# Segment mean on one core: boundaries of the rows from 66 on computed on ScalarE, two check parts moved to ScalarE, own columns placed in two parts

## The chip, the cores and the metric

The kernel runs on one core of a Trainium2 chip. The metric is the time on the device for one execution in microseconds; lower is better. The kernel before takes 188.7 us, the median of four runs (188.03 to 189.13).

## The reference

The input is ten million float32 values and ten million segment numbers (int64), sorted in ascending order, between 0 and 9999. The output is the mean of the values of each of the 10,000 segments:

```
sums = zeros(num_segments); counts = zeros(num_segments)
np.add.at(sums, segment_ids, data)
np.add.at(counts, segment_ids, 1)
return sums / np.maximum(counts, 1)
```

Since the numbers are sorted, a segment is one contiguous piece of the data. With about 1000 values in each, what has to be found is where one segment ends and the next begins, and the sum of the values between two such places.

## The kernel before

Each of the 128 partitions takes 78,125 consecutive values, cut into 90 rows of L = 875 (the last has 250). A row is shorter than a segment usually is, so it holds at most one boundary, and four things are done for it:

- **Probes.** SyncE loads every 175th segment number (`pr`, 8-byte elements, L163), two rows in one transfer. From the sum SG of a row's five probes VectorE finds in which piece of 175 the boundary lies (ST) and the address of that piece (IDX): `first_look`, six instructions for a group of six rows, L284 to L303. The last of them makes YY, the number of probes and their sum in one value.
- **Gather.** GpSimd fetches for each row the 175 numbers of that piece (`GT`, L317), one indirect transfer per row, into a ring of 18 rows. The six gathers of a group are issued as soon as `first_look` has their addresses.
- **Boundary.** ScalarE adds up the gathered numbers (`add_ids`, L327) into G in PSUM. VectorE then makes the boundary's place KK from YY and G (`second_look`, L334). It does this for six rows at once, and from row HALVES = 66 on for three. At the last row it also adds `tl`, which corrects for the shorter last row (L339).
- **Total and split.** ScalarE sums the row's values (`total`, L347), and VectorE sums the values ahead of KK (`split`, L352). Both read the data tile, which holds two rows (875 KB). SyncE loads the tiles, 26 rows ahead, in one queue with the probes (L171). The last tile comes in two transfers (L171, L173).

The order of the work is written out by hand. A loop at the kernel's end (L865 to L897) goes through the rows r. In row r it issues loads that are due; then the boundary sums of the rows up to r + x_sum (6 rows ahead, and 5 from row 66 on) on ScalarE; then `total(r)`, `split(r)`, and whatever the list `after[r]` holds. `put(r, steps, every)` writes steps into this list, `every` of them to a row. All engines run their own instructions in this order, and each waits only for what it needs.

The list holds the rest of the computation in pieces. `counts` turns boundaries into reciprocals of counts (L573 to L591). `sums` makes running sums (L598 to L610). `select` and `table` put the means of a partition's first rows into a table (L662, L671, L676). `place` moves the table's columns to the 79 segments that the partition owns (L686, L693). The columns that later rows reach are found by `pick` (masks, on GpSimd for the later rows: L703 to L718) and `spread` (L748, L751), whose product for rows 62 to 77 runs on GpSimd at L751 and is summed by VectorE at L759, behind row 83. `inject` adds the last two rows.

A check runs along: `check_frame`, `check_windows` (L528 to L532) and `check_columns` fill an array `bad`, `verdict` sums it (L557), adds it over the partitions on TensorE (L558) and makes a flag (L561). All engines load this flag into a register at L850, which stands in the list behind row 80. If it is set, a slow general path runs at the end; with this input it doesn't.

Of the kernel before, what the change touches and what calls it, by code (L numbers as in the profile page):

```python
# [17 lines left out]
P = 128  # L18
# [7 lines left out]
W = S  # L26
# [92 lines left out]
def kernel(  # L119
# [24 lines left out]
    def x_sum(r):  # L144
        return 6 if r < HALVES else 5

# [100 lines left out]
    def g_of(a, b):  # L247
        i = [(r // GROUPS[0] if r < HALVES else 1 + (r - HALVES) // 3) % 2 for r in range(a, b)]
        assert min(i) == max(i)
        return G[i[0]][:, a:b]  # L250
# [18 lines left out]
    def first_look(g):  # L269
# [28 lines left out]
        def s5():  # L298
            for c, d, w in [(a, b - 1, S), (b - 1, b, TAIL)] if last else [(a, b, S)]:
                v.scalar_tensor_tensor(  # L300
                    out=IDX[:, c:d], in0=ST[:, c:d], scalar=float(w), in1=wb[:, c:d], op0=ALU.mult, op1=ALU.add
                )
            v.scalar_tensor_tensor(  # L303
                out=YY[:, a:b], in0=ST[:, a:b], scalar=float(K + 1), in1=SG[:, a:b], op0=ALU.mult, op1=ALU.add
            )
            if last:
                v.tensor_scalar(
                    out=tl, in0=ST[:, NR - 1 : NR], scalar1=-1.0, scalar2=float(TAIL - S),
                    op0=ALU.add, op1=ALU.mult,
                )  # L310
            gather(g)
# [13 lines left out]

    def add_ids(r):
        nc.scalar.activation(  # L327
            out=junk_a, in_=gt32[:, r % RING, 0 : 2 * W : 2], func=ACT.Copy,
            accum_out=g_of(r, r + 1),
        )  # L330

    def second_look(a, b):
        def s1():
            nc.vector.scalar_tensor_tensor(  # L334
                out=KK[:, a:b], in0=YY[:, a:b], scalar=float(S // K), in1=g_of(a, b),
                op0=ALU.mult, op1=ALU.subtract,
            )
            if b == NR:
                nc.vector.tensor_add(out=KK[:, NR - 1 : NR], in0=KK[:, NR - 1 : NR], in1=tl)  # L339

        return [s1]
# [60 lines left out]
    bads = cpool.tile([P, 1], FP32, name="bads")  # L402
    badi = cpool.tile([P, 1], I32, name="badi")
    misc = ppool.tile([P, 512], FP32, name="misc")
    ext = misc[:, 0 : 5 * E + 1]
# [119 lines left out]
    def check_windows():  # L525
# [4 lines left out]
            ),  # L530
            lambda: v.tensor_mul(out=j2, in0=j1, in1=j1),
            lambda: v.scalar_tensor_tensor(  # L532
# [22 lines left out]
    def verdict():  # L555
        def s1():
            nc.vector.tensor_reduce(out=bads, in_=bad, axis=AX.X, op=ALU.add)  # L557
            nc.tensor.matmul(out=badp, lhsT=ones, rhs=bads, start=True, stop=True)  # L558
# [239 lines left out]
    for a, b in zip(bounds[1:], bounds[2:]):  # L798
        if a < HALVES:
            put(a - 1, second_look(a, b))  # L800
        else:
            put(a - 1, second_look(a, a + 3))
            put(a + 2, second_look(a + 3, b))
    for g in range(HEAD, NG):
# [3 lines left out]
    def mixed(p, q):  # L808
# [23 lines left out]
    put(59, counts(Q1, R1), 2)  # L832
    put(R1 - 1, mixed(sums(Q1, R1), select(H1, M1)) + table(H1, M1, tab), 2)
    put(64, place(0, T1, tab, [(0, C1, ND + 1, OUT[:, 0:C1]), (C1, T1, ND + 1, xa[:, 0 : T1 - C1, RM - R1])]))
    look = bounds[NG - 1] - X_LOOK - 2
# [9 lines left out]
    put(look + 1, edges_of(RE, NR))  # L845
    put(look + 4, single(0, NX, bad[:, NX:NC]) + verdict())
    put(look + 4, [
# [6 lines left out]
        + total_of(xa[:, C2 - C1 :, :], add[:, 0 : CA - C2, nb]))  # L854
    w = weights()
    put(RS - 2, counts(RM, R2) + w[:3], 99)
    block = sums(RM, R2, False, RS) + spread(RM, R2, pb, add[:, :, 0:nb], NO - C2) + total_of(add, most)
# [71 lines left out]
```

## Time and profile before

| | us |
|---|---|
| median of four runs | 188.7 |
| the profiled execution's own time | 187.97 |
| its span in the profile | 186.2 |
| VectorE (DVE) busy | 141.2 (76%) |
| ScalarE (ACT) busy | 116.9 (63%) |
| GpSimd (POOL) busy | 99.9 (54%) |
| splits, L352, 90 of them, mean 1118 ns | 100.6 |
| totals, L347, 90 of them, mean 931 ns | 83.8 |
| boundary sums, L327, 90 of them, mean 333 ns | 29.9 |
| gathers, L317, 90 of them, mean 1010 ns | 90.9 |

DMA moved 54.63 MB, a mean of 293 GB/s. The span is what the profile shows between the first and the last instruction; the execution's own time also has what lies around it. The profile cuts the span into 40 slices of equal length and gives for each the busy share of each engine in tenths. A line of the timeline gives start, length, engine, line, operation, tiles with their shapes, and in brackets how long the engine had been idle and what seems to have ended that. The reading out of a sum (READ_ACCUMULATOR) is an instruction of its own behind the one that sums. A busy share is a mean over stages, so the prediction takes the stages one by one.

### The profile page before, as it was taken

The numbers are of one execution on the slowest core, as the hardware profiler recorded it, in microseconds if no ns is written. First come the engines' busy times: TensorE is split into PE (matmuls) and PEld (weight loads), VectorE is DVE, ScalarE is ACT, GpSimd is POOL, SyncE is SP. The second block draws the span as 40 slices with busy tenths as digits, with TensorE's granted clock in tenths as the row PEclk, the third lists the DMA queues.
The fourth block names the chain that finished last, engine by engine and source line by source line (L and its number), as shares of the span: only waits on it lengthen the run. The fifth ranks groups of instructions, "written<-read, shape, count | busy, mean of one in ns | idle before, by whom it ended". The sixth has DMA issues, their size and how long they took to land.

```text
span 186.2 us, 1477 instructions
## 1 busy us (share of the span) xinstructions
PE 1.6 (1%) x6; PEld 1.4 (1%) x6; DVE 141.2 (76%) x438; ACT 116.9 (63%) x362; POOL 99.9 (54%) x119
## 2 busy tenths in 40 slices
PE   0000000000002000000000000000000000010000
PEld 0000000000001000000000000000000000010000
DVE  6522397989297697757799997567699989999991
ACT  8010488935988293873928748397585485959920
POOL 5578776086725728275282664707527478784000
DMA  6899999999999999999999999999998999999100
GB/s 31 175 154 351 336 330 329 316 330 328 330 327 301 340 341 308 322 321 322 330 306 333 328 330 314 298 344 305 325 279 232 330 403 403 410 405 399 60 0 12
DMA packets 70613, 54.63 MB, mean 293 GB/s; under 512 B 60464, under 2 KB 61032, under 8 KB 70599
## 3 DMA queue, kind: packets, MB, share of 16 engines
q1 hardware_dynamic: 64667, 40.50, 74.4%
q0 software_dynamic: 5760, 14.01, 23.0%
q14 instruction: 14, 0.11, 0.2%
q10 hardware_dynamic: 172, 0.00, 0.1%
HBM read 56.59 MB, written 0.04 MB: 304 GB/s over the span
## 4 chain that ended last, share of the span: by engine, by line
SPq 34%; DMA 23%; DVE 16%; issue 13%; POOL 7%; ACT 3%; POOLq 0%; ACTq 0%; DVEq 0%
SPq L171 26%; DMA GT<-in_segment_ids_dram,IDX 14%; DMA data_t<-in_data_dram 10%; DVE junk_v L352 8%; SPq L163 8%; POOL GT L317 6%; ACT junk_t L347 2%; ACT junk_a L327 1%; POOL xa L751 1%; DVE sel L671 1%; DVE shf L686 1%; POOL pb L717 0%; DVE ct L585 0%; DVE most L759 0%; DVE sel L662 0%
## 5 line engine op out<-in xcount | busy, mean ns | idle before, releaser
L317 POOL DMA_INDIRECT GT<-in_segment_ids_dram,IDX x90 | 90.9, 1010 | 67.4 <-ACT junk_a L327 33.8
L352 DVE SCALAR_TENSOR_TENSOR junk_v<-iota,q,data_t 128x875 bf16<-128x875 f32 x90 | 100.6, 1118 | 15.9 <-DMA data_t<-in_data_dram 14.5
L347 ACT ACTIVATE junk_t<-data_t 128x875 bf16<-128x875 f32 x90 | 83.8, 931 | 3.2 <-DMA data_t<-in_data_dram 2.8
L327 ACT ACTIVATE junk_a<-GT 128x175 f32<-128x175 int32 x90 | 29.9, 333 | 57.3 <-DMA GT<-in_segment_ids_dram,IDX 51.9
L347 ACT ACTIVATION_READ_ACCUMULATOR junk_t<-data_t 128x1 f32 x90 | 15.6, 174 | 0.0
L327 ACT ACTIVATION_READ_ACCUMULATOR junk_a<-GT 128x1 f32 x90 | 12.5, 139 | 0.0
L334 DVE SCALAR_TENSOR_TENSOR q<-YY,G 128x6 f32<-128x6 f32 (+1 forms) x19 | 2.9, 155 | 12.4 <-ACT junk_a L327 12.4
L352 DVE DVE_READ_ACCUMULATOR junk_v<-iota,q,data_t 128x1 f32 x90 | 7.4, 82 | 0.0
L284 DVE TENSOR_REDUCE SG<-pr 128x6 f32<-128x30 int32 x15 | 2.7, 180 | 5.3 <-DMA pr<-in_segment_ids_dram 5.2
L293 DVE TENSOR_SCALAR far<-ST 128x6 f32<-128x6 f32 x15 | 2.9, 195 | 0.5
L187 ACT ACTIVATE GT<-q 128x3150 int32<-128x3150 f32 x1 | 3.0, 2994 | 0.0
L300 DVE SCALAR_TENSOR_TENSOR IDX<-ST,wb 128x6 int32<-128x6 f32 (+2 forms) x16 | 2.6, 165 | 0.5
L296 DVE TENSOR_TENSOR ST<-ST,far 128x6 f32<-128x6 f32 x15 | 2.6, 170 | 0.5
L287 DVE SCALAR_TENSOR_TENSOR ST<-pr,SG 128x6 f32<-128x6 int32 x15 | 2.5, 166 | 0.5
L303 DVE SCALAR_TENSOR_TENSOR YY<-ST,SG 128x6 f32<-128x6 f32 x15 | 2.5, 168 | 0.0
L236 DVE CAST jj<-jj_i 128x128 f32<-128x128 int32 x1 | 1.5, 1483 | 0.7 <-POOL jj_i L235 0.7
L598 DVE TENSOR_TENSOR q<-T,q 128x44 f32<-128x44 f32 (+3 forms) x4 | 0.7, 174 | 1.7 <-ACT junk_t L347 1.6
L187 ACT ACT_TABLE_LOAD x1 | 1.3, 1283 | 0.7 <-PEq L913 0.7
L718 POOL TENSOR_SCALAR pb<-pb 128x168 f32<-128x168 f32 (+1 forms) x2 | 1.6, 784 | 0.2
L558 PE MATMUL misc<-bads,ones 128*128 128x1 f32 x2 | 0.6, 363 | 104.7 <-DVE bads L557 104.7
L558 PEld LDWEIGHTS misc<-bads,ones 128*128 128x128 f32 x2 | 0.5, 312 | 104.7 <-DVE bads L557 104.7
L585 DVE RECIPROCAL ct<-ct 128x16 f32<-128x16 f32 (+2 forms) x4 | 1.2, 300 | 0.1
(129 smaller groups left out, 44.9 us busy)
## 6 DMA issues: line engine op xcount, KB each, us to landing
data_t<-in_data_dram SPq DMA_DIRECT2D x44, 875.0 KB, 10.4
GT<-in_segment_ids_dram,IDX POOLq DMA_INDIRECT x90, 6.4
pr<-in_segment_ids_dram SPq DMA_DIRECT2D x41, 10.0 KB, 8.0
data_t<-in_data_dram SPq DMA_DIRECT2D x1, 437.5 KB, 18.6
data_t<-in_data_dram SPq DMA_DIRECT2D x1, 125.0 KB, 15.9
out_dram<-OUT SPq DMA_DIRECT2D x1, 36.6 KB
pr<-in_segment_ids_dram SPq DMA_DIRECT2D x1, 31.0 KB, 4.0
snt<-in_segment_ids_dram ACTq DMA_DIRECT2D x1, 1.0 KB
```

The lines of the kernel that those rows point to most:

```text
L163: nc.sync.dma_start(out=pr_flat[:, a:b], in_=ids_p[:, a * S : (b - 1) * S + 1 : S])
L171: nc.sync.dma_start(out=d[:, 0 : c - a], in_=data_p[:, a:c])
L187: nc.scalar.activation(out=gt32[:, :, 0 : 2 * W : 2], in_=view(q5[:, 0, 0:1], [[0, RING], [0, W]]), func=ACT.Copy)
L284: v.tensor_reduce(out=SG[:, a:b], in_=pr32[:, a:b, 0 : 2 * K : 2], axis=AX.X, op=ALU.add)
L293: v.tensor_scalar(out=far, in0=ST[:, a:b], scalar1=0.0, scalar2=FAR, op0=ALU.is_equal, op1=ALU.mult)
L296: v.tensor_add(out=ST[:, a:b], in0=ST[:, a:b], in1=far)
L300: v.scalar_tensor_tensor(out=IDX[:, c:d], in0=ST[:, c:d], scalar=float(w), in1=wb[:, c:d], op0=ALU.mult, op1=ALU.add)
L317: nc.gpsimd.indirect_dma_start(out=GT[:, r % RING, :], out_offset=None, in_=ids2d[:], in_offset=bass.IndirectOffsetOnAxis(ap=IDX[:, r : r ...
L327: nc.scalar.activation(out=junk_a, in_=gt32[:, r % RING, 0 : 2 * W : 2], func=ACT.Copy, accum_out=g_of(r, r + 1),)
L334: nc.vector.scalar_tensor_tensor(out=KK[:, a:b], in0=YY[:, a:b], scalar=float(S // K), in1=g_of(a, b), op0=ALU.mult, op1=ALU.subtract,)
L347: nc.scalar.activation(out=junk_t[:, 0:n], in_=d, func=ACT.Copy, accum_out=t)
L352: nc.vector.scalar_tensor_tensor(out=junk_v[:, 0:n], in0=iota[:, 0:n], scalar=KK[:, r : r + 1], in1=d, op0=ALU.is_lt, op1=ALU.mult, accum_ ...
```

## The change

- From row 66 on, ScalarE computes KK by itself: an activation with factor -1 and the bias YY of that row, whose sum over the 175 elements is written to KK. YY is made to fit in `first_look` by another operation of the same size. The second looks of these rows are gone, and the sums stand 4 rows ahead instead of 5. The addition of `tl` becomes a step of its own, ahead of the last `counts`.
- The square in `check_windows` and the sum of `bad` in `verdict` go from VectorE to ScalarE. The last step of the verdict (the flag) moves from behind row 79 to behind row 80, directly ahead of the register load.
- The columns of the first table are placed in two parts: 23 of them behind rows 50 and 51, the other 33 behind rows 65 and 66. Before, all 56 were placed behind rows 64 and 65.
- `select` of windows 5 to 7 goes from behind row 61 to behind row 60, and the sums and table of rows 44 to 61 begin behind row 62 instead of row 61.

```diff
--- before.py
+++ after.py
@@ -142,7 +142,7 @@
     ctx.enter_context(tc.manual_schedule())
 
     def x_sum(r):
-        return 6 if r < HALVES else 5
+        return 6 if r < HALVES else 4
 
 
     pr = cpool.tile([P, NR + 1, K], I64, name="pr")
@@ -245,7 +245,7 @@
     T = [ppool.tile([P, 512], FP32, name=f"T{i}") for i in range(2)]
 
     def g_of(a, b):
-        i = [(r // GROUPS[0] if r < HALVES else 1 + (r - HALVES) // 3) % 2 for r in range(a, b)]
+        i = [r // GROUPS[0] % 2 for r in range(a, b)]
         assert min(i) == max(i)
         return G[i[0]][:, a:b]
 
@@ -300,9 +300,12 @@
                 v.scalar_tensor_tensor(
                     out=IDX[:, c:d], in0=ST[:, c:d], scalar=float(w), in1=wb[:, c:d], op0=ALU.mult, op1=ALU.add
                 )
-            v.scalar_tensor_tensor(
-                out=YY[:, a:b], in0=ST[:, a:b], scalar=float(K + 1), in1=SG[:, a:b], op0=ALU.mult, op1=ALU.add
-            )
+            if a < HALVES:
+                v.scalar_tensor_tensor(
+                    out=YY[:, a:b], in0=ST[:, a:b], scalar=float(K + 1), in1=SG[:, a:b], op0=ALU.mult, op1=ALU.add
+                )
+            else:
+                v.tensor_add(out=YY[:, a:b], in0=ST[:, a:b], in1=VI[:, a + 1 : b + 1])
             if last:
                 v.tensor_scalar(
                     out=tl, in0=ST[:, NR - 1 : NR], scalar1=-1.0, scalar2=float(TAIL - S),
@@ -324,6 +327,12 @@
             )
 
     def add_ids(r):
+        if r >= HALVES:
+            nc.scalar.activation(
+                out=junk_a, in_=gt32[:, r % RING, 0 : 2 * W : 2], func=ACT.Identity,
+                scale=-1.0, bias=YY[:, r : r + 1], accum_out=KK[:, r : r + 1],
+            )
+            return
         nc.scalar.activation(
             out=junk_a, in_=gt32[:, r % RING, 0 : 2 * W : 2], func=ACT.Copy,
             accum_out=g_of(r, r + 1),
@@ -335,8 +344,6 @@
                 out=KK[:, a:b], in0=YY[:, a:b], scalar=float(S // K), in1=g_of(a, b),
                 op0=ALU.mult, op1=ALU.subtract,
             )
-            if b == NR:
-                nc.vector.tensor_add(out=KK[:, NR - 1 : NR], in0=KK[:, NR - 1 : NR], in1=tl)
 
         return [s1]
 
@@ -401,6 +408,7 @@
     nbl = cpool.tile([P, 2], FP32, name="nbl")
     bads = cpool.tile([P, 1], FP32, name="bads")
     badi = cpool.tile([P, 1], I32, name="badi")
+    badj = cpool.tile([P, 2 * NX + 8], FP32, name="badj")
     misc = ppool.tile([P, 512], FP32, name="misc")
     ext = misc[:, 0 : 5 * E + 1]
     badp = misc[:, 5 * E + 1 : 5 * E + 2]
@@ -528,7 +536,7 @@
             lambda: v.scalar_tensor_tensor(
                 out=j1, in0=KEY[:, PAD : PAD + NX], scalar=-8.0, in1=ur, op0=ALU.mult, op1=ALU.add
             ),
-            lambda: v.tensor_mul(out=j2, in0=j1, in1=j1),
+            lambda: nc.scalar.activation(out=j2, in_=j1, func=ACT.Square),
             lambda: v.scalar_tensor_tensor(
                 out=bad[:, 0:NX], in0=j2, scalar=21.75 * 21.75, in1=BT[:, 0:NX], op0=ALU.is_gt, op1=ALU.mult
             ),
@@ -554,7 +562,7 @@
 
     def verdict():
         def s1():
-            nc.vector.tensor_reduce(out=bads, in_=bad, axis=AX.X, op=ALU.add)
+            nc.scalar.activation(out=badj, in_=bad, func=ACT.Copy, accum_out=bads)
             nc.tensor.matmul(out=badp, lhsT=ones, rhs=bads, start=True, stop=True)
 
         def s2():
@@ -798,9 +806,6 @@
     for a, b in zip(bounds[1:], bounds[2:]):
         if a < HALVES:
             put(a - 1, second_look(a, b))
-        else:
-            put(a - 1, second_look(a, a + 3))
-            put(a + 2, second_look(a + 3, b))
     for g in range(HEAD, NG):
         if g < NG - 1:
             put(max(bounds[g] - X_LOOK, 0), first_look(g), 5)
@@ -830,8 +835,11 @@
     put(52, [lambda: nc.sync.dma_start(out=out2d[0:SHIFT, :].rearrange("n u -> u n"), in_=tab[0:1, 0:SHIFT])])
     put(58, keys(48, 72)[1:], 2)
     put(59, counts(Q1, R1), 2)
-    put(R1 - 1, mixed(sums(Q1, R1), select(H1, M1)) + table(H1, M1, tab), 2)
-    put(64, place(0, T1, tab, [(0, C1, ND + 1, OUT[:, 0:C1]), (C1, T1, ND + 1, xa[:, 0 : T1 - C1, RM - R1])]))
+    put(R1 - 2, select(H1, M1))
+    put(R1, sums(Q1, R1) + table(H1, M1, tab), 2)
+    CF = 7 * H1 - ND + 1
+    put(50, place(0, CF, tab, [(0, CF, ND + 1, OUT[:, 0:CF])]))
+    put(65, place(CF, T1, tab, [(CF, C1, ND + 1, OUT[:, CF:C1]), (C1, T1, ND + 1, xa[:, 0 : T1 - C1, RM - R1])]))
     look = bounds[NG - 1] - X_LOOK - 2
     put(46, check_frame(), 2)
     put(66, check_windows())
@@ -843,7 +851,8 @@
     put(look + 2, counts(R1, RM), 2)
     put(look, pick(nc.gpsimd, pb[:, :, RE - RM :], C2, NO - C2, RE, R2), 99)
     put(look + 1, edges_of(RE, NR))
-    put(look + 4, single(0, NX, bad[:, NX:NC]) + verdict())
+    put(look + 4, single(0, NX, bad[:, NX:NC]) + verdict()[:1])
+    put(look + 7, verdict()[1:])
     put(look + 4, [
         lambda: v.tensor_scalar(out=nbl, in0=BT[:, NR - 2 : NR], scalar1=-1.0, scalar2=None, op0=ALU.mult)
     ])
@@ -853,6 +862,7 @@
     put(RM + 5, total_of(xa[:, 0 : C2 - C1, :], OUT[:, C1:C2])
         + total_of(xa[:, C2 - C1 :, :], add[:, 0 : CA - C2, nb]))
     w = weights()
+    put(RS - 2, [lambda: v.tensor_add(out=KK[:, NR - 1 : NR], in0=KK[:, NR - 1 : NR], in1=tl)])
     put(RS - 2, counts(RM, R2) + w[:3], 99)
     block = sums(RM, R2, False, RS) + spread(RM, R2, pb, add[:, :, 0:nb], NO - C2) + total_of(add, most)
     put(RS - 1, mixed(block, w[3:]), 99)
```

## The prediction

> **What bounds the kernel now.** I read the page's slices first, to see which resource is full when.
>
> ```profile
> DVE  6522397989297697757799997567699989999991
> ACT  8010488935988293873928748397585485959920
> POOL 5578776086725728275282664707527478784000
> DMA  6899999999999999999999999999998999999100
> GB/s 31 175 154 351 336 330 329 316 330 328 330 327 301 340 341 308 322 321 322 330 306 333 328 330 314 298 344 305 325 279 232 330 403 403 410 405 399 60 0 12
> ```
>
> A slice is 4.66 us. DMA is full from slice 2 to slice 36 (about 172 us), so up to there rows come as fast as they are transferred. The one dip is at 279 and 232 GB/s (slices 29 and 30, 135 to 144 us). Behind slice 36 only VectorE works. The table by stages sizes the dip:
>
> ```profile
> 138.00:142.00 4.00, 0.00 (x0) 0.00 (x0) 3.97 (x9) 2.79 (x11) 2.91 (x3) 1.00 0.86 130
> 152.00:172.00 20.00, 0.59 (x2) 0.50 (x2) 18.55 (x59) 15.42 (x49) 14.93 (x18) 1.00 1.02 405
> ```
>
> The last columns are DMA share and GB/s: 0.86 against 1.07 to 1.09 in its neighbours (packets overlap, so "full" is over 1). About 4 x 0.2 = 0.8 us of transfer time is lost there.
>
> Next, VectorE's timeline: the start of a split (L352) against the landing of its tile. The DMA view of one issue gives the landing: rows 72/73 issued 142.45 + 10.2 = 152.65; rows 80/81 147.18 + 16.8 = 163.98; rows 86/87 152.73 + 20.0 = 172.73. The semaphore for rows 68/69 had its last count at 144.97. Splits of rows 68, 72, 80 and 86 start at 145.06, 152.76, 164.72 and 172.92. A waiting split starts 0.09 to 0.11 us behind its landing (68, 72), so row 86 could have started at 172.83: VectorE is 0.1 us behind the data there, and at row 80 0.6.
>
> ```profile
> 152.76 1.13 DVE L352 SCALAR_TENSOR_TENSOR junk_v<-iota,q,data_t 128x875 bf16<-128x875 f32 x1 [0.81 <-DMA data_t<-in_data_dram]
> ...
> 169.99 0.40 DVE L759 TENSOR_REDUCE OUT<-xa 128x14 f32<-128x238 f32 x1 [0.33 <-POOL xa L751]
> ...
> 172.92 1.13 DVE L352 SCALAR_TENSOR_TENSOR junk_v<-iota,q,data_t 128x875 bf16<-128x875 f32 x1
> 173.97 0.08 DVE L352 DVE_READ_ACCUMULATOR junk_v<-iota,q,data_t 128x1 f32 x1
> 173.97 0.15 DVE L334 SCALAR_TENSOR_TENSOR q<-YY,G 128x3 f32<-128x3 f32 x1
> 174.16 0.16 DVE L339 TENSOR_TENSOR q<-q,tl 128x1 f32<-128x1 f32 x1
> 174.35 0.18 DVE L573 TENSOR_TENSOR ps<-q,QQ 128x16 f32<-128x16 f32 x1
> ```
>
> The middle line is a third bound: the reduce behind row 83 waited 0.33 us for GpSimd. GpSimd's timeline shows why:
>
> ```profile
> 149.31 1.00 POOL L317 DMA_INDIRECT GT<-in_segment_ids_dram,IDX  x1 [2.74 <-ACT junk_a L327]
> ...
> 158.69 1.10 POOL L317 DMA_INDIRECT GT<-in_segment_ids_dram,IDX  x1 [0.17 <-issue]
> ...
> 168.72 1.24 POOL L751 TENSOR_TENSOR xa<-pa,RG 128x528 f32<-128x528 f32 x1
> ```
>
> From the gather of row 78 on, GpSimd has no wait but its 0.30 us between gathers: two sets of six (1.3 us each), two picks, one product, 20.65 us to 169.96. Its start is not ScalarE's doing, as the bracket says: VectorE's indices for rows 78 to 83 (L300, behind row 69) end at 148.55, and gathers of the two groups before also start 0.76 us behind theirs. So data of row 68, 3.5 us of VectorE, 0.76, then 20.65 us of GpSimd set the reduce behind row 83, and 2.93 us later row 86 starts. Three chains (transfer, VectorE, GpSimd) reach row 86 within 0.1 us. Behind it there is VectorE alone, 13.3 us to the end.
>
> **What the Trainium skill says.** *ScalarE: Activation LUTs*, "What ACT_TABLE_LOAD costs": 186 ns + 0.833 ns per element with immediate operands, about 93 ns more for a pointer operand. The trace agrees for 175 elements: 332 by the formula, 333 measured. *DMA: Bandwidth & Descriptors*, "Latency and other measured facts", gives a register load from memory a floor of about 600 ns; the trace has 547 ns on VectorE's sequencer (L850). *Advanced Engine Details and Errata*, "Sequencer Loop", says other instructions can be queued while such a control instruction runs; no run here shows it for one that follows its own input at once. *DMA: Bandwidth & Descriptors*, "Queues, rings and completion order": each DMA engine alternates between queues by packet; the trace shows gathers and data sharing time, but a gather takes 6.4 us to land.
>
> **The change part by part.**
>
> *Second looks gone (eight of 128x3, 0.15 us each).* In the pipeline one costs 0.07 us (146.12 to 146.19). Those before row 86 only let VectorE wait for data or GpSimd. The last, behind row 86, leads a dependent chain, so its whole step goes: 174.16 - 173.97 = 0.19 us. The addition of tl stays in its place.
>
> *ScalarE's boundary sums.* Bias from a tile: an estimate of 333 + 93 = 426 ns, x 24 rows = 2.2 us on ScalarE; at the other end nothing. They come one row later (4 ahead, not 5), but each serves its row alone. ScalarE was 2 rows behind VectorE at row 80 only since the sum of 5 rows ahead waited for its gather. Worked forward from the landings (row 85 at 167.0), at 1.4 us per row it ends row 89's sum at about 173.5, 0.5 us before VectorE adds tl at 174.0. Cover gone, the excess would go straight to the end. No second table load stands in the built program.
>
> *Check parts.* Squaring leaves VectorE between rows 67 and 68 (0.2 us, then it waits for row 68's data). The check's sum (0.38 us) leaves it behind row 78: 1.43 to 1.17 us for that row, 0.26 saved. ScalarE takes two pieces of an estimated 0.28 and 0.53 us, queued ahead of sums needed over 4 us later.
>
> *Verdict a row later.* It now stands directly ahead of the register load. Before, the load ran beside row 80's split. Now VectorE does badi (0.15), the load (0.55), then the scan: bounds 0 and 0.75 us; I take 0.75. With 0.5 us saved in rows 72 to 80 it reaches row 83's end at about 169.8, still before GpSimd's 169.9. So it is covered, by 0.1 us.
>
> *Placing in two parts, sums of rows 44 to 61 behind row 62.* 23 of 56 columns go to rows 50 and 51: two instructions, about 0.4 us each, 0.45 us of it ahead of the indices for rows 60 to 65, where VectorE then waits on data (1.34 us at row 58). Behind row 65 it saves about 0.7 us, again into a wait. The sums waited 1.60 us on ScalarE's row 61 (L598). That row's total no longer queues behind the gather wait of row 66's sum, and the sums come a row later, so the wait goes: row 62 starts at 132.75 instead of 134.26 and the indices for rows 72 to 77 come 1.4 us earlier. Their six gathers reach the queues at 137.1, not 138.48. That fills some of the dip, but the tile of rows 68/69 is behind the same engines.
>
> **The sum.** Row 68 starts with its data, as before. Row 69 and the indices 0.07 us earlier (one second look), so GpSimd's product and row 86 0.07 earlier; behind it 0.19. Together 0.26 us: the profiled execution goes from 187.97 (span 186.20, 1.77 around it) to 187.7. It lies 0.73 under the median of 188.7, so the median goes to 188.44; for what earlier gathers may take from row 68 I round up to 188.5. Tells of no change on this kernel end at 0.5%, 0.94 us.
>
> **Rivals.** *The dip is filled and row 68 comes earlier.* With gathers of rows 72 and 73 gone from under its last packets (they landed at 141.84 and 146.06), tile 68/69 could land up to 0.8 us earlier, all that the dip lost; GpSimd's chain and the data of row 86 follow: 188.44 - 0.8 = 187.6. For: two DMA slices under 300 GB/s. Against: that tile waits behind the last loads of 8-byte ids in its own queue, which gathers don't shorten.
>
> *Slower: the gathers go ahead of that tile.* Three more gathers of 179 KB at 405 GB/s are 0.44 us each, 1.3 us in front of row 68; it moves GpSimd's whole chain, 188.44 + 1.3 = 189.7. It decides from 0.26 us on, little more than half a gather. For: engines alternate by packet. Against: from 139.5 to 142 us they have free time.
>
> *The register load isn't covered.* If VectorE stands 1.2 us rather than 0.75, row 83 ends 0.35 late: 188.8.
>
> *VectorE was the bound all along*, and its removed work counts: about 0.8 us in rows 72 to 86 without the load, 0.05 net with it, so 188.4: not to be told from the first.
>
> **How the numbers follow.** Forecast (with the last two) 0.60, 188.1 to 188.9; filled dip 0.22, 187.5 to 188.1; gathers ahead 0.18, 188.8 to 189.7. Faster by over 0.5% (under 187.76) takes 0.17 of the filled dip and 0.04 of an uneven measurement, 0.21; slower (over 189.64) 0.17, with ScalarE late at row 89 included; the rest 0.62. The range 187.5 to 189.6 leaves out the far ends of both.
>
> **What would show it.** Right: row 68's split still starts with its landing near 145; row 62 waits for data, not for ScalarE; the reduce behind row 83 waits for GpSimd by a few tenths; a hole of about 0.7 us behind row 80 on VectorE; row 86 at 172.8; 13.1 us from there. Wrong: row 86 off by more than 0.5 us, its data landing well before 172, or a wait on ScalarE at tl's addition.

## The result and the profile after

The changed kernel took 189.36 us in the median of 42 runs, from 187.81 to 192.45; the kernel before, in 63 runs beside it, 188.66 us. The ratio is 1.0029, with a 95% interval of 1.0011 to 1.0047: slower by 0.29%, or 0.55 ± 0.32 us in the means. That is less than the 0.5% at which the prediction drew its line, but it has the other sign than the small gain that was forecast. The profiled execution took 189.1 us, its span 187.3 instead of 186.2.

Executions over 1.5% slower than the fastest of their kernel are left out of every ratio and mean, and the profiles of experiments 1, 2, 6, 7 and 16 caught such ones, so no position in time is taken from these five, and a wait or a distance in them is an indication only.

Slices of the kernel after, 4.68 us each:

```profile
DVE  6522397979286777757899998568888699987991
...
POOL 5577776176726637175272654707548068785000
...
GB/s 28 177 148 345 333 329 328 312 326 338 322 329 308 329 334 316 328 321 329 313 313 329 322 331 312 339 316 304 307 281 264 332 410 399 407 394 391 8 0 12
```

The dip (slices 29 and 30) is a little shallower, 281 and 264 GB/s instead of 279 and 232. The table by stages says the same of the stretch in which the gathers now start:

```profile
138.00:142.00 4.00, 0.00 (x0) 0.00 (x0) 3.53 (x8) 3.02 (x9) 3.08 (x4) 1.00 0.93 185
```

The DMA share is 0.93 instead of 0.86, and 185 GB/s instead of 130. The stream is about 0.9 us later in this execution, and in the window moved along with it (138.90 to 142.90) the share is 0.93 as well, at 148 GB/s. So something did fill the dip, as one rival said, and the kernel is slower all the same. VectorE's timeline says where the time went. Before, row 68 and the indices of rows 78 to 83 stood here:

```profile
145.06 1.13 DVE L352 SCALAR_TENSOR_TENSOR junk_v<-iota,q,data_t 128x875 bf16<-128x875 f32 x1
...
148.38 0.17 DVE L300 SCALAR_TENSOR_TENSOR IDX<-ST,wb 128x6 int32<-128x6 f32 x1
```

And after:

```profile
146.48 1.13 DVE L359 SCALAR_TENSOR_TENSOR junk_v<-iota,q,data_t 128x875 bf16<-128x875 f32 x1 [1.76 <-DMA data_t<-in_data_dram]
...
149.73 0.17 DVE L300 SCALAR_TENSOR_TENSOR IDX<-ST,wb 128x6 int32<-128x6 f32 x1
...
166.56 0.28 DVE L612 TENSOR_TENSOR_SCAN FFP<-NBP,FFP,XX 128x16 f32<-128x16 f32 x1 [0.67 <-DVE badi L569]
...
171.26 0.40 DVE L767 TENSOR_REDUCE OUT<-xa 128x14 f32<-128x238 f32 x1 [0.92 <-POOL xa L759]
...
174.24 1.13 DVE L359 SCALAR_TENSOR_TENSOR junk_v<-iota,q,data_t 128x875 bf16<-128x875 f32 x1
...
175.29 0.16 DVE L865 TENSOR_TENSOR q<-q,tl 128x1 f32<-128x1 f32 x1
```

From top to bottom: row 68 waits 1.76 us for its data and starts at 146.48, not 145.06. The indices of rows 78 to 83 end at 149.90, not 148.54. The register load leaves a hole of 0.67 us. The reduce behind row 83 waits 0.92 us for GpSimd, not 0.33. Row 86 starts at 174.24, not 172.92. And the last line stands directly behind the reading of row 86's split: the second look is gone from between. GpSimd's timeline:

```profile
150.66 0.99 POOL L320 DMA_INDIRECT GT<-in_segment_ids_dram,IDX  x1 [5.31 <-issue]
...
169.99 1.24 POOL L759 TENSOR_TENSOR xa<-pa,RG 128x528 f32<-128x528 f32 x1
```

Its chain is as long as before: 150.66 to 171.22 is 20.56 us, against 20.65. It starts 1.35 us later, and row 86 is 1.32 later. VectorE was done with row 83 at 170.34, and the data of row 86 landed at 172.82: in this execution GpSimd alone sets row 86. Without its wait of 0.92 us VectorE would have reached row 86 at 173.32 (an estimate), which is still 0.50 behind the data. From row 86's start to VectorE's last instruction it takes 8.96 us instead of 9.15, so the saving behind row 86 is 0.19, as forecast. 1.32 - 0.19 = 1.13 us is the difference of the two spans.

Why is the tile of rows 68/69 later? By the last counts of their semaphores, tiles landed at these times (us):

| tile | before | after | difference |
|---|---|---|---|
| rows 50/51 | 109.62 | 110.27 | 0.65 |
| rows 66/67 | 140.74 | 141.63 | 0.89 |
| rows 68/69 | 144.97 | 146.36 | 1.39 |

The first 0.65 us was there ahead of anything that the change moves, so it is no effect of it: in the profiles of the other kernels (experiment 4 and the five named above apart), which don't differ up to there, the same tile landed from 109.43 to 111.01. What added the 0.24 us up to the tile of rows 66/67 stays open. The last 0.50 us is from that tile to the next. The DMA view of just that stretch, 140.74 to 144.97 before and 141.63 to 146.36 after, has for the queue of the gathers (packets, MB, share):

```profile
q0 software_dynamic: 82, 0.20, 13.5%
```

```profile
q0 software_dynamic: 120, 0.30, 17.5%
```

Half as much again of the gathers' bytes goes between the two tiles (and 1.00 MB instead of 0.92 on the queue of the tiles themselves). The first three gathers of rows 72 to 77 were issued before the tile of rows 66/67 landed, and the fourth 0.12 us behind it; before, two were, and the fourth came 2.2 us behind it. At the 275 GB/s of that stretch the 0.10 MB more is an estimated 0.36 us.

The 0.50 us comes from one pair of profiles. The same distance between the two tiles is 4.12 us in experiment 13, whose gathers come as late as before, counted from the tile of rows 66/67, and 4.36 and 4.45 us in experiments 5 and 17, whose gathers come about as early as in the change. So earlier gathers go with a later tile in all three, but by 0.1 to 0.5 us, and how much of that the gathers themselves do isn't settled.

### The profile page after: what moved, and what is told of

Read it like the earlier page. It is cut to its first block, busy times and chain, and to the rows that moved or that the text cites. A ratio compares the mean times of both kernels' runs of the same rounds, so it can differ in the third digit from the quotient of the medians.

```text
span 187.3 us, 1478 instructions
## 1 busy us (share of the span) xinstructions
PE 1.6 (1%) x6; PEld 1.4 (1%) x6; DVE 140.1 (75%) x430; ACT 119.7 (64%) x365; POOL 99.0 (53%) x119
## 5 line engine op out<-in xcount | busy, mean ns | idle before, releaser
L336 ACT ACTIVATE junk_a<-GT 128x175 f32<-128x175 int32 x66 | 21.9, 332 | 47.2 <-DMA GT<-in_segment_ids_dram,IDX 43.3
L331 ACT ACTIVATE junk_a<-GT,YY 128x175 f32<-128x175 int32 x24 | 9.9, 414 | 3.7 <-DMA GT<-in_segment_ids_dram,IDX 3.7
L343 DVE SCALAR_TENSOR_TENSOR q<-YY,G 128x6 f32<-128x6 f32 x11 | 1.7, 158 | 11.9 <-ACT junk_a L336 11.9
L336 ACT ACTIVATION_READ_ACCUMULATOR junk_a<-GT 128x1 f32 x66 | 9.2, 139 | 0.0
L331 ACT ACTIVATION_READ_ACCUMULATOR junk_a<-GT,YY 128x1 f32 x24 | 4.6, 192 | 0.0
L304 DVE SCALAR_TENSOR_TENSOR YY<-ST,SG 128x6 f32<-128x6 f32 x11 | 1.8, 166 | 0.0
L612 DVE TENSOR_TENSOR_SCAN FFP<-NBP,FFP,XX 128x16 f32<-128x16 f32 (+2 forms) x4 | 1.1, 270 | 0.7 <-DVE badi L569 0.7
```

The lines of the kernel that those rows point to most:

```text
L304: v.scalar_tensor_tensor(out=YY[:, a:b], in0=ST[:, a:b], scalar=float(K + 1), in1=SG[:, a:b], op0=ALU.mult, op1=ALU.add)
L331: nc.scalar.activation(out=junk_a, in_=gt32[:, r % RING, 0 : 2 * W : 2], func=ACT.Identity, scale=-1.0, bias=YY[:, r : r + 1], accum_out=K ...
L336: nc.scalar.activation(out=junk_a, in_=gt32[:, r % RING, 0 : 2 * W : 2], func=ACT.Copy, accum_out=g_of(r, r + 1),)
```

## The experiments

The theory to test: gathers that are issued earlier go ahead of the tile of rows 68/69, and GpSimd's unbroken chain hands this delay to row 86. The rivals: the hole at the register load; ScalarE's longer sums; or only the place that the stream has in one execution.

**1. The gathers of row 72 held back.** The change, with 128x420 of idle work on GpSimd ahead of the gather of row 72 (its input is filled once, behind the gathers of group 4):

```diff
+            if g == 12:
+                nc.gpsimd.tensor_scalar(
+                    out=fill[:, 0:420], in0=fill[:, 0:420], scalar1=ST[:, b - 1 : b], scalar2=None, op0=ALU.mult
+                )
...
```

> The changed kernel, with one filler on GpSimd (128 x 420 float32, about 1.4 us by the 0.93 us that its 128 x 280 pick takes) ahead of the gather of row 72, so that the six gathers of rows 72 to 77 start about where they did before the change. GpSimd theory (the earlier gathers put the tile of rows 68/69 back, which starts GpSimd's chain late, which sets row 86): the tile of rows 68/69 lands about 3.3 us behind that of 66/67 minus nothing lost to gathers (4.2 us, not 4.7), the reduce behind row 83 waits 0.3 us or less, and the ratio to the kernel before falls from 1.003 to 0.999 (about 0.7 us). Register load theory (the hole behind row 80 costs the time): stays at 1.003, since the filler doesn't touch it.

Ratio to before 1.0021 (0.9994 to 1.0048). Between the two answers, so it decides nothing.

**2. The indices of rows 78 to 83 a row earlier.** The change, with that first look behind row 68 instead of 69:

```diff
-            put(max(bounds[g] - X_LOOK, 0), first_look(g), 5)
+            put(max(bounds[g] - X_LOOK, 0) - (g == 13), first_look(g), 5)
```

> The changed kernel, with the first look of rows 78 to 83 behind row 68 instead of row 69, so that GpSimd's chain of gathers, picks and product starts one row (about 1.3 us) earlier. GpSimd theory: the reduce behind row 83 waits 0 to 0.2 us instead of 0.92, row 86 starts within 0.3 us of its data, and the ratio to the kernel before is 0.997 to 0.999. Register load theory: no change, 1.003.

1.0007 (0.9971 to 1.0042). The wait for GpSimd behind row 83 is gone from the profile (0.00 instead of 0.92). The interval reaches from a gain to the change's own ratio, so the time decides nothing.

**3. The sums' order alone.** The kernel before, with only the order of select, sums, table and place changed, and the place in one part:

```diff
-    put(R1 - 1, mixed(sums(Q1, R1), select(H1, M1)) + table(H1, M1, tab), 2)
-    put(64, place(0, T1, tab, [...]))
+    put(R1 - 2, select(H1, M1))
+    put(R1, sums(Q1, R1) + table(H1, M1, tab), 2)
+    put(65, place(0, T1, tab, [...]))
```

> The kernel before, with one part of the change alone: select of windows 5 to 7 behind row 60, sums and table of rows 44 to 61 from row 62 on, their placing a row later. GpSimd theory: row 62 waits for data and no more for ScalarE, the indices of rows 72 to 77 come about 1.4 us earlier, the tile of rows 68/69 later, the reduce behind row 83 waits over 0.7 us, ratio 1.003 to 1.004 (nothing of the change's gain behind row 86 is in it). Register load theory: the load is beside row 80's split as before, ratio 1.000 or below.

1.0027 (1.0000 to 1.0055). In the profile row 68 starts at 145.95 and the reduce behind row 83 waits 0.86 us for GpSimd. That is what the theory expected, but not by its route. Row 62 waited 0.56 us instead of 1.60, and yet it started no earlier than before (134.26):

```profile
134.50 1.13 DVE L352 SCALAR_TENSOR_TENSOR junk_v<-iota,q,data_t 128x875 bf16<-128x875 f32 x1 [0.56 <-DVE RB L589]
```

The gathers of rows 72 to 77 reached the queue at 138.66, not before the 138.48 of the kernel before. So in this execution it wasn't an earlier start of the gathers that made row 68 late, and the experiment neither supports the theory nor refutes it.

**4. GpSimd's chain lengthened.** The kernel before, with 128x300 of idle work on GpSimd ahead of the gather of row 78:

```diff
+            if g == 13:
+                nc.gpsimd.tensor_scalar(
+                    out=fill[:, 0:300], in0=fill[:, 0:300], scalar1=ST[:, b - 1 : b], scalar2=None, op0=ALU.mult
+                )
...
```

> The kernel before, with a filler on GpSimd (128 x 300 float32, about 1.0 us) between the indices of row 78 and its gather. GpSimd theory: its chain was within 0.1 us of setting row 86, so nearly all of the filler appears: the wait of the reduce behind row 83 goes from 0.33 to 1.3 us, the end moves by 0.9 us, ratio 1.0045 to 1.005. If VectorE or the transfers set row 86: below 1.001.

1.0090 (1.0058 to 1.0123), 1.74 ± 0.38 us: the direction of it held, the size was missed by nearly double. GpSimd's timeline, then VectorE's reduce behind row 83:

```profile
149.38 1.62 POOL L313 TENSOR_SCALAR fill<-fill,ST 128x300 f32<-128x300 f32 x1 [1.83 <-DVE ST L297]
151.17 1.08 POOL L324 DMA_INDIRECT GT<-in_segment_ids_dram,IDX  x1 [0.17 <-issue]
```

```profile
171.87 0.40 DVE L766 TENSOR_REDUCE OUT<-xa 128x14 f32<-128x238 f32 x1 [0.87 <-POOL xa L758]
```

The gather of row 78 starts 1.78 us behind the end of its indices (149.39) instead of 0.77, so the filler cost 1.01 us. The indices themselves end 0.85 later, behind a row 62 that waited 2.32 us for ScalarE instead of 1.60; whether that comes with the edit or with the execution isn't shown. Together 1.86; row 86 starts 1.87 us later than before, at 174.79, though its data landed at 172.91. The filler's 1.01 us lies below the whole measured interval, so GpSimd's chain has no slack: what is put on it goes to the end whole. Where the rest of the 1.74 comes from in the mean is not shown.

**5. The hole taken out.** The change, with the verdict in one piece, as before:

```diff
-    put(look + 4, single(0, NX, bad[:, NX:NC]) + verdict()[:1])
-    put(look + 7, verdict()[1:])
+    put(look + 4, single(0, NX, bad[:, NX:NC]) + verdict())
```

> The changed kernel, with the verdict's flag again behind row 79 instead of directly ahead of the register load behind row 80; the check's sum stays on ScalarE. GpSimd theory (GpSimd's chain sets row 86): the hole of 0.67 us behind row 80 closes and the wait of the reduce behind row 83 grows from 0.9 to about 1.6 us; the time stays at 1.003 of the kernel before. Register load theory: the time falls by most of 0.7 us, to 0.999 to 1.000.

1.0011 (0.9976 to 1.0046), which holds both answers. No hole stands in the profile any more. VectorE takes 16.55 us from row 72's start to row 83's end instead of 17.32, and stands still for GpSimd instead:

```profile
170.10 0.40 DVE L767 TENSOR_REDUCE OUT<-xa 128x14 f32<-128x238 f32 x1 [0.87 <-POOL xa L759]
```

**6. Experiments 2 and 5 in one.**

> The changed kernel, with both: the flag behind row 79 again and the first look of rows 78 to 83 behind row 68. If the two chains (GpSimd's, and VectorE's with the hole behind row 80) each hold row 86 back, then neither edit alone gains all, and together row 86 starts within 0.2 us of its data; ratio to the kernel before 0.996 to 0.998. If the transfers alone hold it: 1.000 or more, as for the early look alone (1.0007).

1.0004 (0.998 to 1.0028): the expected gain is missed. With both supposed brakes gone the change is still not measurably faster than before, so a third thing may be behind them. Experiments 10 to 15 look for it.

**7. The loads of 8-byte ids kept apart.** The change, with two of these loads, which stood one behind the other on SP's queue ahead of a tile, moved apart:

```diff
-        while pnext < NR and pnext <= r + X_PIECE + pnext // bounds[NG - 1] + X_DATA:
+        while pnext < NR and pnext <= r + X_PIECE + X_DATA:
```

> The changed kernel, with the probe loads of rows 82/83 and 84/85 no longer back to back on SyncE: the tile of rows 68/69 is issued between them (the look-ahead of probes doesn't grow by one at row 84). Theory that the tile of rows 68/69 is the first link (tile, VectorE's indices for row 78, GpSimd's chain, row 86): it lands over 1.5 us earlier against the tile of rows 66/67, GpSimd's chain starts over 1 us earlier, the wait of the reduce behind row 83 is gone; then VectorE with its hole, or the data of row 86, set it; ratio 0.997 to 1.000. Rival that the whole transfer stream sets the end: below 0.997, if the dip at 140 us fills as well, since all landings move by 0.5 us or more; or 1.003, if nothing else moves.

1.003 (1.0003 to 1.0058): the expected gain, 0.997 to 1.000, is missed. In the profile (an indication only) the tile of rows 68/69 lands 3.07 us behind that of rows 66/67 instead of 4.73, and the reduce no longer waits for GpSimd. None of that reaches the end, so an earlier tile of rows 68/69 alone doesn't mend the change. What it lost instead wasn't followed up.

**8. Gathers earlier still.** The kernel before, with the first look of rows 72 to 77 two rows earlier, and nothing else:

```diff
-            put(max(bounds[g] - X_LOOK, 0), first_look(g), 5)
+            put(max(bounds[g] - X_LOOK, 0) - 2 * (g == 12), first_look(g), 5)
```

> The kernel before, with the first look of rows 72 to 77 two rows earlier (behind row 61), so that their six gathers start about 4 us earlier and stand ahead of the tile of rows 68/69. Theory that earlier gathers put this tile back: it lands 5 to 6 us behind that of rows 66/67 instead of 4.2, GpSimd's chain starts 1 us or more later, ratio 1.004 or more. Rival (gathers only fill the dip in the transfers): the distance of the tiles stays or shrinks, the ratio is 1.000 or below.

1.0065 (1.0039 to 1.0092), as the theory expected. The dose is larger than the change's: the gathers reach the queue at 134.03 instead of 138.48, 4.45 us earlier, where the change has 137.85, 0.63 us earlier. The gathers' queue between the landings of the tiles of rows 66/67 and 68/69 (141.63 to 146.47), then VectorE:

```profile
q0 software_dynamic: 130, 0.31, 18.7%
```

```profile
146.57 1.13 DVE L352 SCALAR_TENSOR_TENSOR junk_v<-iota,q,data_t 128x875 bf16<-128x875 f32 x1 [2.08 <-DMA data_t<-in_data_dram]
...
171.41 0.40 DVE L759 TENSOR_REDUCE OUT<-xa 128x14 f32<-128x238 f32 x1 [0.97 <-POOL xa L751]
```

It is the change's picture without the change: row 68 late, the wait for GpSimd 0.97 us, row 86 at 174.34. And the stream as a whole is quicker: the data of row 86 landed at 171.66, 1.05 us sooner than before (0.86 counted from the tile of rows 50/51), and lies there for 2.7 us until VectorE comes.

**9. The same, with GpSimd's chain released.** Experiment 8 with the first look of rows 78 to 83 two rows earlier as well, so that it no longer stands behind the late tile:

```diff
-            put(max(bounds[g] - X_LOOK, 0) - 2 * (g == 12), first_look(g), 5)
+            put(max(bounds[g] - X_LOOK, 0) - 2 * (g in (12, 13)), first_look(g), 5)
```

> The kernel before, with the first looks of rows 72 to 77 and of rows 78 to 83 both two rows earlier. The first alone cost 0.65% (the six gathers ahead of the tile of rows 68/69) although all data from row 72 on came up to 1 us earlier. GpSimd theory: with the second look behind row 67, GpSimd's chain hangs no longer on the tile of rows 68/69, so the loss is gone and the earlier data count: the reduce behind row 83 doesn't wait, row 86 starts within 0.3 us of its data, ratio 0.994 to 0.998. Rival (early gathers cost by their load on the transfers as such): the loss stays, 1.004 or more.

0.9986 (0.9952 to 1.0019). The loss of experiment 8 is gone; the two intervals don't meet. The gain that was expected on top, 0.994 to 0.998, isn't established.

```profile
146.13 1.13 DVE L352 SCALAR_TENSOR_TENSOR junk_v<-iota,q,data_t 128x875 bf16<-128x875 f32 x1 [0.92 <-DMA data_t<-in_data_dram]
...
168.57 0.39 DVE L759 TENSOR_REDUCE OUT<-xa 128x14 f32<-128x238 f32 x1
169.15 1.13 DVE L352 SCALAR_TENSOR_TENSOR junk_v<-iota,q,data_t 128x875 bf16<-128x875 f32 x1 [0.18 <-DMA data_t<-in_data_dram]
```

Row 68 is as late as in the others, and it doesn't matter: its bracket says data, but nothing on GpSimd hangs on it any more, and the reduce waits for nobody.

**10. The change with both looks earlier and the hole out.** The edits of 5 and 9 on the change.

> The changed kernel, with three edits: the flag behind row 79 again, and the first looks of rows 72 to 77 and of rows 78 to 83 two rows earlier. If GpSimd's chain from row 69 on, and then VectorE's hole behind row 80, are all that held the change back, row 86 starts with its data, 1 us earlier than in the kernel before, and the 0.19 us behind it come on top: last VectorE instruction near 181, ratio 0.993 to 0.997. If only the transfers count: 0.999 or more.

1.0013 (0.9981 to 1.0044): missed. The data of row 86 landed at 173.72 in its profile, 0.9 later than in the change's.

**11. ScalarE's boundary sums alone.** The kernel before, with the first part of the change's list only (sums by bias and factor, second looks gone, `tl` added by itself), the sums still 5 rows ahead.

```diff
+        if r >= HALVES:
+            nc.scalar.activation(
+                out=junk_a, in_=gt32[:, r % RING, 0 : 2 * W : 2], func=ACT.Identity,
+                scale=-1.0, bias=YY[:, r : r + 1], accum_out=KK[:, r : r + 1],
+            )
+            return
...
-        else:
-            put(a - 1, second_look(a, a + 3))
-            put(a + 2, second_look(a + 3, b))
```

> The kernel before, with one part of the change alone: KK of the rows from 66 on comes from ScalarE with bias and factor, 5 rows ahead as before, second looks gone; check, placing and the order of sums as before. The step of 0.19 us behind row 86 is saved, the wait of row 62 for ScalarE stays at 1.5 us or so, so the gathers of rows 72 to 77 keep their place: ratio 0.998 to 1.000. If the sums with a bias (414 ns against 332) make ScalarE late, the addition of tl waits, or rows from 84 on do: 1.001 or more.

1.0027 (0.9998 to 1.0056): the gain doesn't show. VectorE's timeline behind row 86 does get its 0.19 us (8.96 from row 86's start to its last instruction). But:

```profile
170.25 0.40 DVE L767 TENSOR_REDUCE OUT<-xa 128x14 f32<-128x238 f32 x1 [0.80 <-POOL xa L759]
```

VectorE is done with row 83 at 169.45 instead of 169.59, and GpSimd's product at 170.22 instead of 169.96, since its chain began 0.35 us later, behind a row 62 that waited 2.45 us for ScalarE instead of the expected 1.5. So what the second looks saved ahead of row 84 goes into this wait, which was 0.33 before.

**12 and 13. Only the indices of rows 78 to 83 two rows earlier**, in the change (12) and in the kernel before (13):

```diff
-            put(max(bounds[g] - X_LOOK, 0), first_look(g), 5)
+            put(max(bounds[g] - X_LOOK, 0) - 2 * (g == 13), first_look(g), 5)
```

> The changed kernel, with one edit: the first look of rows 78 to 83 two rows earlier, behind row 67, so that GpSimd's chain no longer hangs on the tile of rows 68/69. If the change's loss of 0.55 us goes through this chain, the reduce behind row 83 doesn't wait any more and the ratio to the kernel before falls from 1.003 to 0.998 to 1.000; VectorE's hole behind row 80 stays and may keep up to half a microsecond. If the loss is in ScalarE's longer sums or in the transfers: it stays at 1.003.

> The control: the kernel before, with the same edit alone, the first look of rows 78 to 83 behind row 67. In its profile GpSimd's chain, VectorE and the data of row 86 were within 0.1 us of each other, so the edit should bring next to nothing: ratio 0.998 to 1.000. If it brings as much as in the changed kernel (0.4% or more), GpSimd's chain was a loss that both kernels have, and the change's own loss lies elsewhere.

1.0053 (1.0029 to 1.0077) and 1.0013 (0.9985 to 1.004): both missed, the first clearly. VectorE in experiment 12:

```profile
154.70 1.13 DVE L359 SCALAR_TENSOR_TENSOR junk_v<-iota,q,data_t 128x875 bf16<-128x875 f32 x1 [0.42 <-DMA data_t<-in_data_dram]
...
168.10 0.42 DVE L612 TENSOR_TENSOR_SCAN FFP<-NBP,FFP,XX 128x16 f32<-128x16 f32 x1 [0.68 <-DVE badi L569]
...
171.95 0.40 DVE L767 TENSOR_REDUCE OUT<-xa 128x14 f32<-128x238 f32 x1
...
174.92 1.13 DVE L359 SCALAR_TENSOR_TENSOR junk_v<-iota,q,data_t 128x875 bf16<-128x875 f32 x1
```

Nobody waits for GpSimd. But the gathers of rows 78 to 83 now go ahead of the tiles of rows 70 to 76: row 72 starts at 154.70, not 153.02. And from row 72 on VectorE is the bound: it needs 20.2 us from row 72's start to row 86's, while the data of row 86 lands 19.3 us behind that of row 72. So VectorE is 1.08 us behind the data at row 86. In experiment 13 it is 20.1 against 19.6, and VectorE 0.60 us behind. This fits as the third thing behind experiments 6 and 10: a fourth chain, VectorE from row 72 on, hardly shorter than GpSimd's.

**14. Experiments 9 and 11 together**, on the kernel before.

> A version that may beat both: the kernel before with KK from ScalarE for the rows from 66 on, and both first looks (rows 72 to 77 and 78 to 83) two rows earlier. Nothing of the check, the placing or the order of sums is changed. Both looks alone gave 0.9986; the step of 0.19 us behind row 86 comes on top: ratio 0.995 to 0.999. If ScalarE's sums with a bias cost as such: 1.000 or more.

0.9979 (0.9947 to 1.001). With experiment 9 the best of all; both intervals still reach to just above 1, so a gain isn't established.

**15. Experiment 12 without the hole** (the verdict's diff of experiment 5).

> e12 (the change with the indices of rows 78 to 83 two rows earlier) measured 1.0053, with VectorE 1.08 us behind the data of row 86 and a hole of 0.68 us behind row 80. This is the same kernel with the verdict a row earlier again, so without the hole. If VectorE with its hole is what bound e12, it gains about 0.6 us: 1.001 to 1.003, row 86 within 0.5 us of its data. If the later tiles of rows 70 to 76 alone bound it, nothing changes: 1.0045 to 1.006.

1.0016 (0.9988 to 1.0045), and in VectorE's timeline:

```profile
166.55 0.73 DVE L612 TENSOR_TENSOR_SCAN FFP<-NBP,FFP,XX 128x16 f32<-128x16 f32 x1
...
170.70 0.40 DVE L767 TENSOR_REDUCE OUT<-xa 128x14 f32<-128x238 f32 x1
...
173.90 1.13 DVE L359 SCALAR_TENSOR_TENSOR junk_v<-iota,q,data_t 128x875 bf16<-128x875 f32 x1
```

The scan follows without a gap. Row 86 is 0.50 us behind its data (173.40), not 1.08. Once GpSimd is out of the way, the hole is on the path. (The intervals of 12 and 15 overlap a little; the profile carries this.)

**16. The hole alone**, on the kernel before:

```diff
-    put(look + 4, single(0, NX, bad[:, NX:NC]) + verdict())
+    put(look + 4, single(0, NX, bad[:, NX:NC]) + verdict()[:1])
+    put(look + 7, verdict()[1:])
```

> The kernel before with the verdict split as in the change and nothing else: it gets the hole of 0.67 us behind row 80. VectorE waited 0.33 us for GpSimd behind row 83, so if that covers it in part row 86 moves by 0.3 to 0.4 us: 1.0015 to 1.002. If it is fully covered: 1.000. If nothing covers it: 1.0035.

1.0001 (0.9973 to 1.003). The hole is in the profile with 0.68 us, and no loss shows. With experiment 5 this speaks against the hole as the cause in the change: put in alone or taken out, it moves less than can be measured. (The intervals are about ± 0.003, and a hole that nothing covers was expected at 0.0035, so a part of it could hide there.)

**17. The change with the old order of sums, select and place:**

```diff
-    put(R1 - 2, select(H1, M1))
-    put(R1, sums(Q1, R1) + table(H1, M1, tab), 2)
-    CF = 7 * H1 - ND + 1
-    put(50, place(0, CF, tab, [...]))
-    put(65, place(CF, T1, tab, [...]))
+    put(R1 - 1, mixed(sums(Q1, R1), select(H1, M1)) + table(H1, M1, tab), 2)
+    put(64, place(0, T1, tab, [...]))
```

> The change with the sums of rows 44 to 61, the select and the placing where they stood before, so that row 62 waits for ScalarE again and the gathers of rows 72 to 77 reach the queues near 138.5 us. If the earlier gathers are what the change lost by, the saved 0.19 us behind row 86 is left: 0.998 to 1.000. If the loss comes from elsewhere (the hole, ScalarE's sums), it stays: 1.002 to 1.004.

1.0006 (0.9978 to 1.0033), between the two answers, and its premise fell. Row 62 doesn't wait for ScalarE even so (it starts at 132.91, with its data at 132.89), and the gathers still leave early, at 137.13. With the sums 5 rows ahead, in experiment 11, row 62 did wait. So it is the boundary sums 4 rows ahead instead of 5 that remove row 62's wait, and the sums' new order isn't needed for it. The tile of rows 68/69 lands 4.45 us behind the one before it (4.23 before, 4.73 after), with 0.27 MB of gathers in between.

## Why the prediction was wrong

**The step that failed** is "Row 68 starts with its data, as before", with the indices of rows 78 to 83 "0.07 us earlier", and with it the term for what earlier gathers may take from row 68, for which the sum was rounded up by 0.06 us (188.44 to 188.5). In the profile the indices ended 1.35 us later. In the mean over executions it is less, since 0.65 us of it was the stream's place in that execution. What goes with the earlier gathers is the 0.1 to 0.5 us between the two tiles, less the 0.19 saved behind row 86: a traced loss of 0.3 us at most, against the measured 0.55 ± 0.32. So the sign of the failed term is seen, and its part of the loss stays open. Experiment 8 shows how large such a term can get: 0.65%, about 1.2 us, with gathers 4.45 us earlier.

**The rival that came nearest** is "the gathers go ahead of that tile". Its mechanism is shown by experiments 8 and 9: earlier gathers alone cost 0.65%, and nothing measurable once GpSimd's chain doesn't hang on row 69. That holds for the 4.45 us by which the gathers were moved there; for the 0.63 us of the change it is argued. Its size was put too high, three gathers or 1.3 us; the packets show a little over half a gather more in front of the tile, 0.10 MB. The argument used against it, that the engines "have free time" from 139.5 to 142 us, was true and proved nothing: the dip filled to 0.93, and the tile still came later. *DMA: Bandwidth & Descriptors*, "Queues, rings and completion order", which was cited, says that an engine serves its queues in turns by packet. That a gather queued earlier takes turns from a tile is an inference from it; the 82 packets of gathers that became 120 agree.

**"The dip is filled and row 68 comes earlier"** was half right: filled, and later.

**The chances** didn't fit together: "gathers ahead" had 0.18 for all of 188.8 to 189.7, and a time over 189.64, the last corner of that range, was given 0.17.

**Three chains within 0.1 us** was right as far as it went. Experiment 4 shows GpSimd's without slack. But VectorE is a fourth from row 72 on, 20.0 to 20.5 us to row 86 in the profiles of experiments 9, 10 and 12 to 15. The prediction saw this only as "0.6 behind at row 80" and as a rival that gave the same time. This fits with no release of GpSimd having brought a clear gain.

**The hole** was priced at 0.75 and measured 0.67 us; "covered" came true, by 0.92 us rather than 0.1, but by luck, because GpSimd's chain was 1.35 us late. At its place before, the product would have ended at 169.87, and VectorE would have been done with row 83 at 170.08 (estimates: 171.22 less 1.35, and 170.34 less the 0.26 by which row 72 was later), so 0.2 us would have stood out. The 0.5 us that rows 72 to 80 were to save was too much: from row 72's start to row 83's end VectorE took 16.83 us before and 16.55 without the hole, in experiment 5. *Advanced Engine Details and Errata*, "Sequencer Loop", speaks of other instructions queued while a control instruction runs: where the load follows its own input directly, as here, the next instruction on VectorE still started only after those 0.67 us.

**Behind row 86** the 0.19 us came exactly, here and in experiments 5, 10 and 11. **ScalarE** was priced well, 414 ns measured for the estimated 426, by the groups after:

```profile
L331 ACT ACTIVATE junk_a<-GT,YY 128x175 f32<-128x175 int32 x24 | 9.9, 414 | 3.7 <-DMA GT<-in_segment_ids_dram,IDX 3.7
...
L331 ACT ACTIVATION_READ_ACCUMULATOR junk_a<-GT,YY 128x1 f32 x24 | 4.6, 192 | 0.0
```

The reading behind it was left out of the estimate: 192 ns instead of 139. The addition of `tl` waited for nothing all the same.

**Row 62** lost its wait for ScalarE, as forecast, and for one of the two reasons given (experiment 17). It started 0.57 us earlier, not 1.5, since its data was 0.96 later.

**What stays open** is how the 0.55 us divides. Either of two parts of the change alone gave 1.0027 (experiments 3 and 11), and the change without one or another part gave 1.0004 to 1.0021 (1, 2, 5, 6, 17), all with intervals of about ± 0.003. Earlier gathers can cost time, by experiment 8, and in the change's profile neither the hole nor ScalarE's durations are on the path. That the gathers are the whole of the loss in the change is argued from its profile, not shown, and experiments 7 and 12 don't fit it without further reasons. The boundary sums 4 rows ahead and the check parts on ScalarE were not run alone.

## What to carry over

When a transfer queue is full, an earlier request on one queue can be a later tile on another: ask which compute chain starts from that tile, and price the delay there, even if the stream as a whole ends sooner. Where several chains reach one point within half a microsecond, list all of them first, since freeing one only uncovers the next; a saving counts in full only behind the point where they meet. Take from one pair of profiles how long steps are and what waits for what, and leave their positions aside until another execution shows how far the stream drifts by itself.

## What the runs showed of the hardware

Idle transfer time in front of a tile is no proof that added traffic is free: the DMA share from 138 to 142 us rose from 0.86 to 0.93, and the tile behind it still came 0.50 us later, measured from the tile before it (0.13 and 0.22 us in experiments 5 and 17). In experiment 8, with gathers 4.45 us earlier, the data of row 86 came 1.05 us sooner and the kernel was 0.65% slower. A register load directly behind the instruction that writes its input held VectorE for 0.67 to 0.68 us in the seven profiles that had it so (after, and experiments 1, 2, 7, 12, 16 and 17). A sum on ScalarE with a bias from a tile costs 414 + 192 ns for 175 elements (the sum and the reading of its accumulator), against 332 + 139 without, where the sum also goes to another tile, in PSUM.
